# Keys of an attention layer projected with their dimensions on the partitions and rotated there by a partition shuffle

## The chip, the cores and the metric

The kernel runs on one core of a Trainium2 chip. The metric is the device time of one execution in microseconds (us); before the change the median of three runs is 559.24 us (558.02 to 559.66). Engines are called TensorE (PE; its weight loads are PEld), VectorE (DVE), ScalarE (ACT), GpSimd (POOL) and SyncE (SP).

## The reference

Two decoder layers on x of 256 tokens by 1024, all in float32. Each layer normalises x, multiplies it by one combined weight matrix `w_in` and splits the columns into a linear-recurrence group (8 heads, "HGRN2") and a sparse-attention group (8 query heads, 2 groups of keys and values, 128 dimensions a head). The attention has three branches: over compressed keys (blocks of 32 tokens sent through a small MLP, 15 of them), over selected blocks (`ks`, `vs`) and over a window (`kw`, `vw`). Queries, `ks`, `kw` and the compressed keys get a partial rotary embedding over their first 32 of 128 dimensions:

```python
def partial_rope(x, pos):
    ...
    x1 = xf[..., :half]
    x2 = xf[..., half:ROT_DIM]
    out = jnp.concatenate([x1 * cos - x2 * sin, x2 * cos + x1 * sin, xf[..., ROT_DIM:]], axis=-1)
```

The branches' outputs are gated and added, both groups are multiplied by a SiLU gate, projected by `w_out`, normalised and added to x.

## The kernel before, in words

Every float32 product is made of three single-pass products: each operand is split into a high part (cast to `float32r`) and the rest, and hi x hi, hi x lo and lo x hi are accumulated in PSUM. The weights are streamed through a ring (class `Ring`): SP loads a unit into one of 5 raw buffers, ScalarE makes the high part (L202), VectorE the low part (L203), into 8 pairs of buffers. `ring.done(n)` gives n units back and lets SP load the units that lie 8 further on; their splitting is due 9 us of program time later.

TensorE does one projection group after another (`layers`, from L1075 on): queries; the forget gates of the recurrence (`hgrn_fast`, whose scans over 1024 elements run on VectorE); `kcvc`, the inputs of the compression; `kv_w`, keys and values of the window with the gate logits; `compress` for the keys; `kv_s`, keys and values of the selected blocks; `compress` for the values; then the recurrence's queries, with attention woven in between. `mm_a` (L363) has a token tile (128 tokens) as the stationary operand and up to 512 columns of the weights as the moving one, so the tokens end up on the partitions. `mm_b` (L373) has 128 columns of the weights as the stationary operand and all 256 tokens as the moving one, so the dimensions end up on the partitions.

Smaller steps are put off: `later(lag, fn, channel)` sets a due time, `tick` advances a clock by the time of the matmuls emitted and emits what is due, and `flush` forces a channel out. From the order of emission a list scheduler sets the order of each engine's instructions when the program is built, by a timing model of its own; semaphores make an engine wait for its operands and for a buffer's last reader. PSUM has 8 banks: three for the tag `mm`, two each for `s` and `t`, one for `o`; the banks of a tag are handed out in turn.

Keys, before: `keys` (L545) takes a bank with 128 tokens by 2 groups x 128 dimensions, rotates it into the tile `kst` (`rope`, L384: one ScalarE copy of 96 dimensions a group, four VectorE instructions over the first 32), and 8 us later `turn_k` transposes the two groups on TensorE (L552) and `split_k` (L539) writes the high part `kTh` on ScalarE (L540) and the low part `kTl` on VectorE (L541). Each layer does this four times, for two token tiles and two branches. The compressed keys come out of `second` (L514) with their 15 blocks on the partitions (two matmuls, L519), are rotated and transposed in `third` (L531). `vals` (L558) splits a bank of values into `vhi` and `vlo`.

In `kv_s` (L563) one bank of `mm` takes 256 columns of keys and 256 of values for a token tile. In `kv_w` (L574) a token tile's keys go to an `mm` bank (256 columns), its values and gate logits to an `s` bank (280 columns). In both, the four weight units are given back during the second token tile's last pass. `kcvc` (L468), just ahead of `kv_w`, fills two `mm` banks; for each, two copies on ScalarE (L477) and two subtractions on VectorE (L478) follow, one after the other. `scores` (L598) reads `kTh` and `kTl`.

Of the kernel before, what the change touches and what calls it, by code (L numbers as in the profile page):

```python
# [19 lines left out]
T = 256  # L20
# [14 lines left out]
CTW = 544  # L35
# [9 lines left out]
L3 = 3.0  # L45
LQ = 4.0
LK = 8.0
# [5 lines left out]
def shape_tables():  # L53
# [10 lines left out]
    for scale in (SCALE, 1.0):  # L64
        r = rope(t, scale)
        parts.append(r[:128])
        parts.append(r[128:])
    e = 16 * np.arange(NCMP) + 31
    rc = np.zeros((128, 64), np.float32)
    rc[:NCMP] = rope(e, 1.0)  # L70
    parts.append(rc)
# [21 lines left out]
    return f, f2, m  # L93


def build(ctx, tc, A, out):
# [150 lines left out]
    rope_k = [ct[:, 256 + 64 * a:320 + 64 * a] for a in range(NT)]  # L247
    rope_c = ct[:, 384:448]
    cmask = [ct[:, 448 + 16 * a:464 + 16 * a] for a in range(NT)]
    sel = ct[:, 480:540].rearrange("p (a n) -> p a n", a=2)  # L250
# [22 lines left out]
    def consts2():  # L273
# [3 lines left out]
        nc.sync.dma_start(out=m2, in_=A["ct2"])  # L277
        nc.gpsimd.memset(cm3, 0.0)
# [208 lines left out]
    def compress(l, i, ring, KC):  # L487
# [26 lines left out]
        def second():  # L514
            y2 = tb()
            n = 96 if i else NCMP
            for g in range(G):
                lhs = act3[:, g, :] if i else act[:, g * 15:(g + 1) * 15]
                P.matmul(out=y2[0:n, g * 128:(g + 1) * 128], lhsT=lhs, rhs=w2[:, i, :], start=True, stop=True)  # L519
            y2v = y2[0:n, 0:256].rearrange("p (g d) -> p g d", g=2)  # L520
            if i:
                S.copy(out=vcs[0:96], in_=y2v)
                V.tensor_tensor(out=vcs[32:64], in0=y2v[32:64], in1=vcs[32:64].bitcast(F32), op=OP.subtract)
                return
            kst = sp.tile([128, 2, 128], F32, name="kst", tag="st", bufs=2)
            rope(kst[0:NCMP], y2v, rope_c, 2, 1.0, NCMP)

            def third():
                tp = tb()
                for g in range(G):  # L530
                    P.transpose(out=tp[:, g * 128:g * 128 + NCMP], in_=kst[0:NCMP, g, :],  # L531
                                identity=ident[0:NCMP, 0:NCMP])
                split_k(256, NCMP, tp.rearrange("p (g n) -> p g n", g=4)[:, 0:2, 0:NCMP])

            later(L3, third, "c0")
# [7 lines left out]
    KOFF = ((128, 0), (272, 400))  # L543

    def keys(a, br, ps):  # L545
        kst = sp.tile([128, 2, 128], F32, name="kst", tag="st", bufs=2)
        rope(kst, ps.rearrange("p (g d) -> p g d", g=2), rope_k[a], 2, 1.0)

        def turn_k():
            tp = tb()  # L550
            for g in range(G):
                P.transpose(out=tp[:, g * 128:(g + 1) * 128], in_=kst[:, g, :], identity=ident)  # L552
            o = KOFF[br][a]
            split_k(o, 128, tp[:, 0:256].rearrange("p (g t) -> p g t", g=2))

        later(LK, turn_k, "k")

    def vals(a, br, ps):  # L558
        hi, lo = vhi[:, a, br, :], vlo[:, a, br, :]
        S.copy(out=hi, in_=ps)  # L560
        V.tensor_tensor(out=lo, in0=ps, in1=hi.bitcast(F32), op=OP.subtract)

    def kv_s(ring):  # L563
        un = ring.take(4)
        for a in range(NT):
            ps = mmb()
            for u in range(4):
                mm_a(ps, un[u], u, a, 0, 512)
                if a:
                    ring.done(1)  # L570
            keys(a, 0, ps[:, 0:256])
            vals(a, 0, ps[:, 256:512])

    def kv_w(ring):  # L574
        un = ring.take(4)
        for a in range(NT):
            ps = mmb()
            for u in range(4):
                mm_a(ps[:, 0:256], un[u], u, a, 0, 256)
            keys(a, 1, ps[:, 0:256])  # L580
            ps = sb_()
            for u in range(4):
                mm_a(ps[:, 0:280], un[u], u, a, 256, 280)
                if a:
                    ring.done(1)
            vals(a, 1, ps[:, 0:256])
            S.activation(out=gt[:, a].rearrange("p h b -> p (h b)"), in_=ps[:, 256:280], func=AF.Sigmoid)

    def attend(a, g):
# [8 lines left out]
        def scores(i):  # L598
            flush("c0")
# [17 lines left out]
            else:  # L617
                flush("k")
# [556 lines left out]
```

## Time and profile before

| | |
|---|---|
| median of 3 runs | 559.24 us (558.02 to 559.66) |
| the profiled execution | 558.97 us |
| its span, first to last instruction | 557.2 us |
| TensorE busy | 543.8 us (98%) |
| weight loads | 487.6 us (88%) |
| VectorE busy | 398.8 us (72%) |
| ScalarE busy | 333.0 us (60%) |
| mean granted TensorE clock | 0.995 |

The rows below come from the profiled execution; times in them are microseconds from the start of its span, mean durations of a group nanoseconds. A matmul's row lasts longer than the distance to the next matmul, since they are pipelined: the distance between the starts is what a matmul costs.

### The profile page before, as it was taken

Reading aid. Unit: us, or ns where it says so; the run is one execution under the profiler, and the core shown is the slowest. Engines: PE = TensorE matmul, PEld = TensorE weight load, DVE = VectorE, ACT = ScalarE, POOL = GpSimd, SP = SyncE. Lnnn points to the kernel's source line nnn. Section 1 sums busy time; section 2 is a strip of 40 time slices with the busy share of each in tenths; the row PEclk is TensorE's granted clock in tenths of the full one; section 3 lists DMA queues with packets and bytes.
Section 4 is the critical chain, followed back from the end, with each engine's and each line's share of the span. In section 5 each row is a group of like instructions: output and inputs, shape, how many; then the busy total and the mean of one; then the engine's idle time right before and its main releaser. Section 6 shows DMA issues by size and latency. Waiting matters only on the chain.

```text
span 557.2 us, 9821 instructions
## 1 busy us (share of the span) xinstructions
PE 543.8 (98%) x3675; PEld 487.6 (88%) x3675; DVE 398.8 (72%) x883; ACT 333.0 (60%) x632; POOL 9.6 (2%) x18
## 2 busy tenths in 40 slices
PE   7999999999999999999999999989999999999994
PEld 4889998899888989988888999979988888898884
DVE  4887997889777277563687599888987654866422
ACT  6576537865567685562557763677646768746311
POOL 4000000000000001001000000000000000000000
PEclk9999999999999999999999999999999999999998
DMA  8698548965146158566385755697433622956111
GB/s 302 195 314 257 146 127 266 304 193 152 39 117 190 35 166 291 185 191 188 115 262 162 228 154 152 196 302 256 125 101 84 174 85 63 303 172 200 59 38 44
DMA packets 72197, 96.56 MB, mean 173 GB/s; under 512 B 3383, under 2 KB 49357, under 8 KB 72142
## 3 DMA queue, kind: packets, MB, share of 16 engines
q1 hardware_dynamic: 71854, 95.33, 55.2%
q8 instruction: 31, 0.51, 0.4%
q10 hardware_dynamic: 288, 0.52, 0.2%
q14 instruction: 24, 0.20, 0.1%
HBM read 93.75 MB, written 2.10 MB: 172 GB/s over the span
## 4 chain that ended last, share of the span: by engine, by line
PE 88%; DMA 4%; ACT 3%; DVE 2%; issue 1%; SPq 0%; ACTq 0%; DVEq 0%
PE ps_mm L378 10%; PE ps_mm L380 10%; PE ps_mm L379 10%; PE ps_mm L368 9%; PE ps_mm L369 9%; PE ps_mm L370 9%; PE ps_mm L1005 4%; PE ps_mm L1007 4%; PE ps_mm L1006 4%; DMA raw<-in_w_in 2%; ACT whi L202 2%; PE ps_t L668 2%; DMA raw<-in_cmp_w_v 2%; PE ps_s L608 1%; DVE wlo L203 1%
## 5 line engine op out<-in xcount | busy, mean ns | idle before, releaser
L203 DVE TENSOR_TENSOR wlo<-raw,whi 128x1024 fp32r<-128x1024 f32 (+1 forms) x168 | 203.0, 1223 | 60.7 <-ACT whi L202 56.3
L202 ACT CAST whi<-raw 128x1024 fp32r<-128x1024 f32 (+1 forms) x168 | 174.9, 1052 | 87.9 <-PE ps_mm L379 24.5
L378 PE MATMUL ps_mm<-Hhi,whi 128*128 128x256 f32 x448 | 127.5, 285 | 0.0
L380 PE MATMUL ps_mm<-Hhi,wlo 128*128 128x256 f32 x448 | 125.7, 281 | 0.0
L379 PE MATMUL ps_mm<-Hlo,whi 128*128 128x256 f32 x448 | 125.7, 281 | 0.0
L368 PE MATMUL ps_mm<-whi,Hhi 128*128 128x512 f32 (+1 forms) x256 | 102.0, 399 | 0.7 <-ACT Hhi L355 0.7
L370 PE MATMUL ps_mm<-whi,Hlo 128*128 128x512 f32 (+1 forms) x256 | 98.9, 386 | 0.0
L369 PE MATMUL ps_mm<-wlo,Hhi 128*128 128x512 f32 (+1 forms) x256 | 98.8, 386 | 0.0
L379 PEld LDWEIGHTS ps_mm<-Hlo,whi 128*128 128x128 f32 x448 | 84.5, 189 | 0.1
L378 PEld LDWEIGHTS ps_mm<-Hhi,whi 128*128 128x128 f32 x448 | 84.3, 188 | 0.1
L380 PEld LDWEIGHTS ps_mm<-Hhi,wlo 128*128 128x128 f32 x448 | 84.4, 188 | 0.0
L370 PEld LDWEIGHTS ps_mm<-whi,Hlo 128*128 128x128 f32 x256 | 48.7, 190 | 10.3 <-DVE Hlo L356 0.3
L368 PEld LDWEIGHTS ps_mm<-whi,Hhi 128*128 128x128 f32 x256 | 48.9, 191 | 8.5 <-ACT Hhi L355 1.1
L369 PEld LDWEIGHTS ps_mm<-wlo,Hhi 128*128 128x128 f32 x256 | 49.0, 191 | 7.5 <-DVE wlo L203 0.5
L630 ACT ACTIVATE sB<-ps_s,nm 128x256 f32<-128x256 f32 (+1 forms) x40 | 16.9, 428 | 12.2 <-DVE nm L627 11.5
L627 DVE CUSTOM_DVE_ANT_0 ps_s<-ps_s,cm 128x128 f32<-128x128 f32 (+1 forms) x64 | 22.4, 371 | 1.9 <-PE ps_s L610 0.7
L671 DVE TENSOR_TENSOR sB<-ps_t,sB 128x512 fp32r<-128x512 f32 x12 | 8.3, 688 | 20.1 <-ACT sB L670 20.1
L1005 PE MATMUL ps_mm<-whi,sN 128*128 128x512 f32 x48 | 19.0, 397 | 0.0
L1006 PE MATMUL ps_mm<-wlo,Hhi 128*128 128x512 f32 x48 | 18.9, 395 | 0.0
L1007 PE MATMUL ps_mm<-whi,Hlo 128*128 128x512 f32 x48 | 18.9, 395 | 0.0
L1006 PE MATMUL ps_mm<-wlo,sN 128*128 128x512 f32 x48 | 18.9, 394 | 0.0
L1007 PE MATMUL ps_mm<-whi,sN 128*128 128x512 f32 x48 | 18.9, 394 | 0.0
(299 smaller groups left out, 921.0 us busy)
## 6 DMA issues: line engine op xcount, KB each, us to landing
raw<-in_w_in SPq DMA_DIRECT2D x112, 512.0 KB, 4.5
raw<-in_w_out SPq DMA_DIRECT2D x32, 512.0 KB, 4.3
raw<-in_w_in SPq DMA_DIRECT2D x8, 536.0 KB, 4.1
raw<-in_cmp_w_k SPq DMA_DIRECT2D x16, 256.0 KB, 3.4
raw<-in_cmp_w_v SPq DMA_DIRECT2D x16, 256.0 KB, 3.2
sB<-in_x SPq DMA_DIRECT2D x3, 512.0 KB, 3.6
sB<-in_post_norm SPq DMA_DIRECT2D x2, 512.0 KB, 4.8
xs<-sB SPq DMA_DIRECT2D x4, 256.0 KB, 2.0
```

The costliest lines, as they stand in the source:

```text
L202: S.copy(out=hi, in_=raw)
L203: V.tensor_tensor(out=lo, in0=raw, in1=hi.bitcast(F32), op=OP.subtract)
L368: P.matmul(out=ps, lhsT=hh, rhs=wh, start=k == 0, stop=False)
L369: P.matmul(out=ps, lhsT=hh, rhs=wl, start=False, stop=False)
L370: P.matmul(out=ps, lhsT=hl, rhs=wh, start=False, stop=k == KT - 1)
L378: P.matmul(out=ps, lhsT=wh, rhs=hh, start=k == 0, stop=False)
L379: P.matmul(out=ps, lhsT=wh, rhs=hl, start=False, stop=False)
L380: P.matmul(out=ps, lhsT=wl, rhs=hh, start=False, stop=k == KT - 1)
L627: V.tensor_tensor_reduce(out=sb[b], in0=sb[b], in1=mk[b], scale=-1.0, scalar=3e38, op0=OP.add, op1=OP.min, accum_out=nm[:, i, b:b + 1])
L1005: P.matmul(out=ps, lhsT=hi, rhs=wh, start=first, stop=False)
L1006: P.matmul(out=ps, lhsT=hi, rhs=wl, start=False, stop=False)
L1007: P.matmul(out=ps, lhsT=lo, rhs=wh, start=False, stop=last)
```

## The change

Keys are projected with the weights as the stationary operand, as in `mm_b`, for all 256 tokens at once, and come last in their group, behind the values; the tile lies in PSUM with the dimensions on the partitions. The new `rope_t` rotates its first 32 partitions in place: a `stream_shuffle` swaps the two halves of the 32 partitions into an SBUF tile, two multiplications by tables (`kt`, a new constant input with the dimensions on the partitions) and an addition follow, all on VectorE. `split_k` then splits the whole bank at once. `turn` does this 1.5 us after the group instead of 8. The compressed keys are made by one matmul with `w2` stationary, rotated the same way and split at once. The transposes of keys, their `kst` tiles and `third` are gone. Values of `kv_s` now take one `mm` bank for both token tiles; values and gate logits of `kv_w` take an `mm` bank for each. The units of a group are given back in the keys' second half. `scores` flushes the keys' channel at its start.

```diff
-CTW = 544
+CTW = 352
+KTW = 544
...
-L3 = 3.0
 LQ = 4.0
-LK = 8.0
+LR = 1.5
...
         nc.sync.dma_start(out=m2, in_=A["ct2"])
+        nc.sync.dma_start(out=kt, in_=A["kt"])
...
+    def rope_t(x, tab, n):
+
+        c, s = (t[:, None, :].to_broadcast([32, G, n]) for t in tab)
+        sh = sp.tile([128, 512], F32, name="sh", tag="st", bufs=2)[0:32, 0:G * n].rearrange("p (g n) -> p g n", g=G)
+        V.stream_shuffle(out=sh, in_=x[0:32], mask=SWAP)
+        V.tensor_tensor(out=sh, in0=sh, in1=s, op=OP.mult)
+        V.tensor_tensor(out=x[0:32], in0=x[0:32], in1=c, op=OP.mult)
+        V.tensor_tensor(out=x[0:32], in0=x[0:32], in1=sh, op=OP.add)
+
...
         def second():
             y2 = tb()
...
+            if not i:
+                P.matmul(out=y2[:, 0:G * NCMP], lhsT=w2[:, 0, :], rhs=act, start=True, stop=True)
+                y2v = y2[:, 0:G * NCMP].rearrange("p (g n) -> p g n", g=G)
+                rope_t(y2v, rope_c, NCMP)
+                split_k(kTh[:, :, 256:256 + NCMP], kTl[:, :, 256:256 + NCMP], y2v)
+                return
...
-    def split_k(o, n, src):
-        S.copy(out=kTh[:, :, o:o + n], in_=src)
-        V.tensor_tensor(out=kTl[:, :, o:o + n], in0=src, in1=kTh[:, :, o:o + n].bitcast(F32), op=OP.subtract)
...
+    def split_k(hi, lo, src):
+        S.copy(out=hi, in_=src)
+        V.tensor_tensor(out=lo, in0=src, in1=hi.bitcast(F32), op=OP.subtract)
+
+    def keys(un, br, ring):
+        ps = mmb()
+        for g in range(G):
+            out = ps[:, g * T:(g + 1) * T]
+            for k in range(KT):
+                wh, wl = (t[:, k % 2, g * 128:(g + 1) * 128] for t in un[k // 2])
+                P.matmul(out=out, lhsT=wh, rhs=Hhi[:, :, k, :], start=k == 0, stop=False)
+                P.matmul(out=out, lhsT=wh, rhs=Hlo[:, :, k, :], start=False, stop=False)
+                P.matmul(out=out, lhsT=wl, rhs=Hhi[:, :, k, :], start=False, stop=k == KT - 1)
+                if g and k % 2:
+                    ring.done(1)
+                tick(3 * 256 / 2400.0)
+
+        def turn():
+            rope_t(ps.rearrange("p (g t) -> p g t", g=G), rope_k, T)
+            if br:
+                split_k(kTh[:, :, 272:528], kTl[:, :, 272:528], ps.rearrange("p (g t) -> p g t", g=G))
+            else:
+                hi, lo = (t[:, :, 0:256].rearrange("p g (a t) -> p g a t", a=NT)[:, :, ::-1, :] for t in (kTh, kTl))
+                split_k(hi, lo, ps.rearrange("p (g a t) -> p g a t", g=G, a=NT))
+
+        later(LR, turn, "k")
...
     def kv_s(ring):
         un = ring.take(4)
+        ps = mmb()
         for a in range(NT):
-            ps = mmb()
             for u in range(4):
-                mm_a(ps, un[u], u, a, 0, 512)
-                if a:
-                    ring.done(1)
-            keys(a, 0, ps[:, 0:256])
-            vals(a, 0, ps[:, 256:512])
+                mm_a(ps[:, a * 256:(a + 1) * 256], un[u], u, a, 256, 256)
+        vals(vhi[:, :, 0, :], vlo[:, :, 0, :], ps.rearrange("p (a d) -> p a d", a=NT))
+        keys(un, 0, ring)
 
     def kv_w(ring):
         un = ring.take(4)
         for a in range(NT):
             ps = mmb()
             for u in range(4):
-                mm_a(ps[:, 0:256], un[u], u, a, 0, 256)
-            keys(a, 1, ps[:, 0:256])
-            ps = sb_()
-            for u in range(4):
                 mm_a(ps[:, 0:280], un[u], u, a, 256, 280)
-                if a:
-                    ring.done(1)
-            vals(a, 1, ps[:, 0:256])
+            vals(vhi[:, a, 1, :], vlo[:, a, 1, :], ps[:, 0:256])
             S.activation(out=gt[:, a].rearrange("p h b -> p (h b)"), in_=ps[:, 256:280], func=AF.Sigmoid)
+        keys(un, 1, ring)
...
         def scores(i):
-            flush("c0")
+            flush("c0", "k")
```

## Rows read from the trace of the kernel before

**Rows 1.** The page's parts 1 and 5: TensorE as a whole, one group of weight loads

```profile
PE 543.8 (98%) x3675; PEld 487.6 (88%) x3675; DVE 398.8 (72%) x883; ACT 333.0 (60%) x632; POOL 9.6 (2%) x18
...
L378 PEld LDWEIGHTS ps_mm<-Hhi,whi 128*128 128x128 f32 x448 | 84.3, 188 | 0.1
```

**Rows 2.** Timeline of TensorE, `kv_w` in both layers: start, duration, instruction, [idle before]

```profile
72.18 0.28 PE L368 MATMUL ps_mm<-whi,Hhi 128*128 128x256 f32 x1
...
75.02 0.29 PE L368 MATMUL ps_s<-whi,Hhi 128*128 128x280 f32 x1
...
78.11 0.28 PE L368 MATMUL ps_mm<-whi,Hhi 128*128 128x256 f32 x1
...
340.22 0.28 PE L368 MATMUL ps_mm<-whi,Hhi 128*128 128x256 f32 x1
```

**Rows 3.** Timeline of TensorE, first token tile of `kv_s` in the first layer

```profile
87.98 0.39 PE L368 MATMUL ps_mm<-whi,Hhi 128*128 128x512 f32 x1
...
90.54 0.39 PE L370 MATMUL ps_mm<-whi,Hlo 128*128 128x512 f32 x1
90.78 0.38 PE L552 MATMUL ps_t<-ct,kst 128*128 128x128 f32 x2
...
91.23 0.40 PE L369 MATMUL ps_mm<-wlo,Hhi 128*128 128x512 f32 x1
```

**Rows 4.** Timeline of VectorE: the last split of each `kcvc` bank, both layers

```profile
75.53 0.60 DVE L478 TENSOR_TENSOR sN<-ps_mm,sN 128x256 fp32r<-128x256 f32 x1
...
80.23 0.63 DVE L478 TENSOR_TENSOR sN<-ps_mm,sN 128x256 fp32r<-128x256 f32 x1
...
341.53 0.63 DVE L478 TENSOR_TENSOR sN<-ps_mm,sN 128x256 fp32r<-128x256 f32 x1
...
348.91 0.63 DVE L478 TENSOR_TENSOR sN<-ps_mm,sN 128x256 fp32r<-128x256 f32 x1
```

**Rows 5.** Timeline of TensorE around `third` (L531), inside `compress` for the values

```profile
102.55 0.28 PE L493 MATMUL ps_s<-wlo,sN 128*68 128x256 f32 x1
...
103.81 0.28 PE L493 MATMUL ps_s<-wlo,sN 128*68 128x256 f32 x1
...
370.65 0.28 PE L493 MATMUL ps_s<-wlo,sN 128*68 128x256 f32 x1
372.33 0.27 PE L531 MATMUL ps_t<-ct,kst 15*128 15x15 f32 x2 [1.40 <-ACT whi L202]
...
372.70 0.28 PE L493 MATMUL ps_s<-wlo,sN 128*68 128x256 f32 x1
372.81 0.28 PE L492 MATMUL ps_s<-whi,sN 128*68 128x256 f32 x1
```

**Rows 6.** Timeline of TensorE: the first scores of the first layer

```profile
114.04 0.28 PE L608 MATMUL ps_s<-kTh,q 128*128 128x272 f32 x1
```

**Rows 7.** Timeline of TensorE around the two matmuls of `second` (L519), first layer

```profile
98.22 0.40 PE L370 MATMUL ps_mm<-whi,Hlo 128*128 128x512 f32 x1
...
99.42 0.40 PE L369 MATMUL ps_mm<-wlo,Hhi 128*128 128x512 f32 x1
```

**Rows 8.** Timeline of TensorE: first dense matmuls of the kernel, and its last one

```profile
9.63 0.79 PE L368 MATMUL ps_mm<-whi,Hhi 128*128 128x512 f32 x1 [0.69 <-ACT Hhi L355]
...
15.45 0.63 PE L368 MATMUL ps_mm<-whi,Hhi 128*128 128x512 f32 x1
15.88 0.43 PE L369 MATMUL ps_mm<-wlo,Hhi 128*128 128x512 f32 x1
...
549.42 0.27 PE L1007 MATMUL ps_s<-whi,Hlo 128*128 128x256 f32 x1
```

**Rows 9.** Busy time by stretch: PE, PEld, DVE, ACT, POOL, granted clock, DMA share, GB/s

```profile
551.50:552.00 0.50, 0.00 (x0) 0.00 (x0) 0.50 (x3) 0.00 (x0) 0.00 (x0) 0.84 0.07 16
```

**Rows 10.** Groups of VectorE's instructions by line and shape: count, busy us, mean ns

```profile
L825 DVE TENSOR_TENSOR sB<-ps_mm,sB 128x512 f32<-128x512 f32 x4 | 2.8, 688 | 0.3 <-PE ps_mm L380 0.3
```

**Rows 11.** Timeline of SP's queue: the issue of the constant table

```profile
2.01 0.43 SPq L271 DMA_DIRECT2D ct<-in_ct  x1
```

More of the change, by code (lines that the diff above doesn't have):

```diff
@@ L63, in shape_tables @@
     parts = [np.eye(128, dtype=np.float32)]
[L64 to L67, printed above, removed]
+    r = rope(t, SCALE)
+    parts.append(r[:128])
+    parts.append(r[128:])
     e = 16 * np.arange(NCMP) + 31
-    rc = np.zeros((128, 64), np.float32)
-    rc[:NCMP] = rope(e, 1.0)
-    parts.append(rc)
     for a in range(NT):
@@ L92, in shape_tables @@
     m = np.ascontiguousarray(np.concatenate(ms, axis=1).astype(np.float32))
-    return f, f2, m
+    rows = [r[:, i:i + 32].T for r in (rope(t, 1.0), rope(e, 1.0)) for i in (0, 32)]
+    kt = np.concatenate(rows, axis=1).astype(np.float32)
+    kt = np.ascontiguousarray(np.pad(kt, ((0, 0), (0, KTW - kt.shape[1]))))
+    return f, f2, m, kt
 def build(ctx, tc, A, out):
@@ L246, in build @@
     rope_q = [ct[:, 128 + 64 * a:192 + 64 * a] for a in range(NT)]
[L247 to L250, printed above, removed]
+    cmask = [ct[:, 256 + 16 * a:272 + 16 * a] for a in range(NT)]
+    sel = ct[:, 288:348].rearrange("p (a n) -> p a n", a=2)
+    kt = cp.tile([32, KTW], F32, name="kt")
+    rope_k = (kt[:, 0:256], kt[:, 256:512])
+    rope_c = (kt[:, 512:512 + NCMP], kt[:, 512 + NCMP:512 + 2 * NCMP])
+    SWAP = [(i + 16) % 32 for i in range(32)]
     cm3 = cp.tile([128, 384], BF, name="cm3")
@@ L515, in second @@
             y2 = tb()
-            n = 96 if i else NCMP
-            for g in range(G):
[L518 to L535, printed above, removed]
@@ L537, in compress @@
-        later(L1[i], sums, "c%d" % i)
-    def split_k(o, n, src):
-        S.copy(out=kTh[:, :, o:o + n], in_=src)
-        V.tensor_tensor(out=kTl[:, :, o:o + n], in0=src, in1=kTh[:, :, o:o + n].bitcast(F32), op=OP.subtract)
[L543 to L556, printed above, removed]
@@ L558, in vals @@
-    def vals(a, br, ps):
-        hi, lo = vhi[:, a, br, :], vlo[:, a, br, :]
+            if not i:
[4 more added lines that the diff above has]
+                return
+            for g in range(G):
+                P.matmul(out=y2[0:96, g * 128:(g + 1) * 128], lhsT=act3[:, g, :], rhs=w2[:, i, :], start=True,
+                         stop=True)
@@ new lines, in second @@
+            y2v = y2[0:96, 0:256].rearrange("p (g d) -> p g d", g=2)
+            S.copy(out=vcs[0:96], in_=y2v)
+            V.tensor_tensor(out=vcs[32:64], in0=y2v[32:64], in1=vcs[32:64].bitcast(F32), op=OP.subtract)
+        later(L1[i], sums, "c%d" % i)
+    def split_k(hi, lo, src):
[21 more added lines that the diff above has]
+        later(LR, turn, "k")
@@ L560, in vals @@
+    def vals(hi, lo, ps):
         S.copy(out=hi, in_=ps)
@@ L617, in scores @@
             else:
-                flush("k")
                 qk(ps[:, 0:272], 0, 272)
@@ L1166 @@
     arrays = {n: np.ascontiguousarray(inputs[n]) for n in _INS}
-    arrays["ct"], arrays["ct2"], arrays["lm"] = shape_tables()
+    arrays["ct"], arrays["ct2"], arrays["lm"], arrays["kt"] = shape_tables()
     A = {n: nc.dram_tensor("in_" + n, a.shape, mybir.dt.from_np(a.dtype), kind="ExternalInput").ap()
```

## The prediction

> **What bounds the kernel now.** I read the page first: TensorE is busy for 543.8 of 557.2 us [rows 1]. That figure alone is weak, since a matmul's row (0.28 us) is longer than the distance to the next one, so I went to the timeline of TensorE through the stage that is changed. There the matmuls of 256 columns start 0.118 us apart ((75.02 - 72.18)/24) and those of 280 columns 0.129 us ((78.11 - 75.02)/24 = 3.09/24) [rows 2]; those of 512 columns start 0.233 us apart ((90.54 - 87.98)/11) [rows 3]. So the distance goes with the columns, and between these groups there is no gap. Whatever takes columns or interruptions from TensorE shortens the kernel one for one, and whatever makes TensorE wait lengthens it one for one. VectorE comes second, and locally it is late: in `kv_w`'s stretch it still works off the gate scans when TensorE has long gone on, and gets to the evacuation of the step before only then [rows 4].
>
> **What the change removes.** (a) Eight pairs of 128x128 transposes (`turn_k`, four a layer). One pair: from the start of the matmul before it, 90.54, to the second start after it, 91.23, are 0.69 us; without the pair two distances of 0.233 would stand there, so a pair costs 0.22 us, and eight cost 1.8 us [rows 3].
> (b) The transposes of the compressed keys (`third`) and the wait ahead of them. In the first layer the starts go from 102.55 to 103.81 us where two distances of 0.118 belong: 1.02 us. In the second layer they go from 370.65 to 372.70, a loss of 1.81 us, of which 1.40 is a wait [rows 5]. TensorE no longer has a step there, so both go: 2.8 us. What was late there, the rotation of the compressed keys, is now awaited only by the first scores, which start at 114.04 us [rows 6].
> (c) `second` for the keys runs two matmuls of 128 columns, each in two passes; it becomes one of 30 columns. Today it lifts the distance from 98.22 to the second matmul behind it, 99.42, to 1.20 us, 0.73 more than the plain 0.467 [rows 7]. The new cost lies between nothing and 0.73; half as many passes make me take half, so 0.37 is saved in each layer, 0.7 in both (0 to 1.5).
>
> **What it adds on TensorE.** `kv_s` exchanges 48 matmuls of 512 columns for 96 of 256 in each layer: 96 x 0.118 - 48 x 0.233 = 0.15 us, 0.3 in both layers [rows 2, 3]. `kv_w` keeps its 48 of 256 and 48 of 280 columns in another order. The Trainium skill speaks against this exchange: "TensorE: Matmul & The Clock Gate", section "Back-to-back issue gap", gives about 81 ns for a matmul of 128 columns and about 131 ns for one of 512 in a stream of weight loads and matmuls; put on a line between them (an estimate), 256 columns would take 98 ns, and the exchange would lose some 6 us over both layers. The trace doesn't agree: it shows 118 and 233 ns, very nearly in proportion.
>
> So TensorE's own work falls by 1.8 + 2.8 + 0.7 - 0.3 = **5.0 us**.
>
> **What it turns into a wait.** `kv_w` used to alternate between the `mm` banks (keys) and the `s` banks (values). Now three tiles in a row come from `mm`, which has three banks, handed out in turn. When `kv_w` starts, one of them is free, and the other two hold the output of `kcvc`. They come free when their last split on VectorE (L478) ends, and ScalarE and VectorE take the four steps of each evacuation one by one, behind the scans. These ends stand in the trace: 75.53 + 0.60 = 76.13 and 80.23 + 0.63 = 80.86 us in the first layer, 341.53 + 0.63 = 342.16 and 348.91 + 0.63 = 349.54 in the second [rows 4]. Before, the second `mm` tile began at 78.11 [rows 2] and the third only in `kv_s`, at 87.98 [rows 3], so nobody waited.
> Now, first layer: values of tile 0 from 72.18 for 3.09 us to 75.27; values of tile 1 wait 0.86 us for 76.13 and end at 79.22; keys wait 1.64 us for 80.86. Second layer: start 340.22 [rows 2], values to 343.31 and 346.40 (the bank of 342.16 is free in time), then keys wait 3.14 us for 349.54. Together 5.6 us. The VectorE work ahead of these two splits isn't touched by the change, so I take the times as they are. Bounds: 0, if the order of VectorE's instructions comes out with the splits first, and 5.6.
>
> A further price hangs on it. The clock granted to TensorE falls after a pause: the last matmul starts at 549.42, and the half microsecond from 551.50 is granted 0.84 on average, so it has gone to the lower level (1.2 GHz) some 2.4 us after the last start [rows 8, 9]. A wait of 1.40 us left no such mark: the matmuls right behind it keep their distance [rows 5]. The new wait of 3.1 us is longer than both, those of 0.9 and 1.6 us are near the harmless one. What the lower clock costs until it comes back: nothing at the least; at the most what the start of the kernel shows, where matmuls of 512 columns run 0.43 us apart (15.45 to 15.88), half the pace, from 9.63 to 15.88, which loses 6.25/2 = 3.1 us [rows 8]. I take the middle, 1.55 us, once, for the second layer.
>
> **What is hidden.** Each branch's rotation on VectorE becomes four instructions over 32 partitions and 512 elements, and one split of 512. The nearest row, 128x512 out of PSUM, takes 0.69 us [rows 10], so a branch takes at most 5 x 0.69 = 3.4 us, and with ScalarE's copy about 4. The shuffle itself is in no row: its bounds are nothing and, as I can't exclude it, twice that row, which makes a branch 4.1 us. The Trainium skill ("VectorE: DVE Perf Modes", section "Rules for kernel authors") has about 2400 ns for 2048 elements, an estimate of 0.6 us here; by it the sum stays. The cover is the time from the end of `kv_s` to the first scores: at 102.55 TensorE is already in the `compress` behind `kv_s` [rows 5], the scores start at 114.04 [rows 6], so 11.5 us at least, less 1.5 us of due time. If it were gone, what ran over would stand ahead of the first scores. Behind these steps on VectorE are weight splits of units that TensorE takes after `compress`. The units of `kv_s` are now given back in its last quarter instead of its second half, up to 3 us later; they let loads start whose data are wanted a whole projection group later: nothing. The extra table costs SP one issue of about 0.43 us, as the other table [rows 11], ahead of loads that stand in a queue behind the weight buffers anyway; the other table gets smaller: nothing either, 0.4 us at most if that cover went.
>
> **Sum.** The profiled execution took 558.97 us, its span 557.2; the median of the runs is 559.24, 0.27 above, and I add to the median. -5.0 + 5.6 + 1.55 = +2.2 us: **561.4 us**.
>
> **Rivals.** (1) *The banks come free in time.* The order of VectorE's instructions is set when the program is built; if the two splits of the second `kcvc` half come ahead of the last scan and the products, there's no wait, and 559.24 - 5.0 = 554.2 us is left: faster. For it: the splits wait in VectorE's queue, not for data. Against it: nothing ahead of them changes, and the order was the same kind in both layers [rows 4]. It decides once more than about 3.3 of the 5.6 us of waiting go. Chance 0.30.
> (2) *The wait comes, the clock stays.* 559.24 + 0.6 = 559.9 us. For it: the harmless 1.40 us [rows 5]. Against it: the fall after the last matmul [rows 8, 9]. Chance 0.20.
> (3) *VectorE becomes the bound*: the rotation of `kw`'s keys, 3.4 us, comes ahead of the splits of the last two weight units of `kv_s`, which TensorE now wants sooner, as its 256-column pass goes through a unit in 0.7 us. That would cost up to the 3.4 us in each layer on top of (2), less what the wait has given: about 563 us. Chance 0.04.
> (4) *Short matmuls are bound by their weight loads*: a load lasts 188 ns [rows 1]; if the new 96 a layer ran at that distance, 2 x 96 x (0.188 - 0.118) = 13 us more. Against it: the same form runs at 0.118 now [rows 2]. It's what the skill's figures point to, in a smaller size. Chance 0.02.
> The forecast keeps 0.44.
>
> **The numbers.** About 0.3% (1.7 us) is what a measurement of this kernel can tell from no change, so faster means below 557.6 and slower above 560.9. Faster: rival (1), 0.30. Same: three quarters of (2), and a fifth of the forecast, where the clock costs little, 0.24. Slower: the rest, 0.46. Both signs hold much, so the range spans them: from just under rival (1), 554.0, to just over the wait with the full price of the clock (559.9 + 3.1), 563.2. The forecast's own range is 559.9 to 563.0.
>
> **What would show it.** In the new trace: no transposes of keys; a gap of about 2.5 us in all ahead of the `kv_w` keys' matmuls in the first layer and of about 3 us in the second, released by L478's successor on VectorE; behind the second gap a stretch of the lower clock. Keys' matmuls 0.118 us apart. The scores still begin without a wait. If the gaps are missing and the span is near 552, the step on the banks is wrong; if they stand there and the clock does not fall, only its price is.

## The result and the profile after

After takes 563.16 us (median of 9 executions, 562.03 to 566.86), before 558.55 us (9 executions beside them); the ratio is 1.0085, with a 95% interval from 1.0064 to 1.0106. By the ratio the change costs 4.7 us. The profiled execution of after took 563.62 us, its span 561.8 us, 4.6 more than before.

The page of the kernel after: busy time of each engine [rows 1], and the group of the keys' matmuls.

```profile
PE 541.2 (96%) x3747; PEld 490.2 (87%) x3747; DVE 402.5 (72%) x867; ACT 331.3 (59%) x616; POOL 9.6 (2%) x18
...
L552 PE MATMUL ps_mm<-Hhi,whi 128*128 128x256 f32 x64 | 18.3, 286 | 4.4 <-DVE sN L489 4.4
```

TensorE is busy for 2.6 us less, but its share of the span falls: work went, waits came. The keys' matmuls alone have 4.4 us of idle time ahead of them, ended by the last split of `kcvc` on VectorE (L489, formerly L478). They stand in the timeline of TensorE after, in `kv_w` of both layers (columns as in [rows 2]).

```profile
75.45 0.29 PE L372 MATMUL ps_mm<-whi,Hlo 128*128 128x280 f32 x1
76.57 0.37 PE L370 MATMUL ps_mm<-whi,Hhi 128*128 128x280 f32 x1 [0.83 <-DVE sN L489]
...
79.61 0.29 PE L372 MATMUL ps_mm<-whi,Hlo 128*128 128x280 f32 x1
81.25 0.36 PE L552 MATMUL ps_mm<-Hhi,whi 128*128 128x256 f32 x1 [1.34 <-DVE sN L489]
81.44 0.28 PE L553 MATMUL ps_mm<-Hlo,whi 128*128 128x256 f32 x1
81.56 0.28 PE L554 MATMUL ps_mm<-Hhi,wlo 128*128 128x256 f32 x1
...
348.48 0.29 PE L372 MATMUL ps_mm<-whi,Hlo 128*128 128x280 f32 x1
351.82 0.36 PE L552 MATMUL ps_mm<-Hhi,whi 128*128 128x256 f32 x1 [3.04 <-DVE sN L489]
```

From start to start these three gaps are 1.12, 1.64 and 3.34 us where 0.13 belongs, 5.7 us lost in all. The keys' matmuls that follow are 0.12 us apart. A second kind of wait comes at the third of the first scores, in the same view.

```profile
119.61 0.28 PE L382 MATMUL ps_mm<-Hhi,wlo 128*128 128x256 f32 x1
121.02 0.39 PE L611 MATMUL ps_s<-kTh,q 128*128 128x272 f32 x1 [1.13 <-ACT sN L632]
...
390.16 0.28 PE L382 MATMUL ps_mm<-Hhi,wlo 128*128 128x256 f32 x1
391.99 0.39 PE L611 MATMUL ps_s<-kTh,q 128*128 128x272 f32 x1 [1.55 <-ACT sN L632]
```

It was not there before, where the third scores follow on at once:

```profile
118.64 0.28 PE L380 MATMUL ps_mm<-Hhi,wlo 128*128 128x256 f32 x1
118.76 0.29 PE L608 MATMUL ps_s<-kTh,q 128*128 128x272 f32 x1
...
387.51 0.28 PE L380 MATMUL ps_mm<-Hhi,wlo 128*128 128x256 f32 x1
387.62 0.29 PE L608 MATMUL ps_s<-kTh,q 128*128 128x272 f32 x1
```

The starts of the first matmul of each stage, read from the same timeline, give each stage's length. "Values in `s`" and "rotation later" are variants of after that are told of below (first and twelfth experiment).

| stage, first / second layer, us | before | after | values in `s` | and rotation later |
|---|---|---|---|---|
| `kv_w` | 11.99 / 12.11 | 14.48 / 15.13 | 11.85 / 11.85 | 11.85 / 11.85 |
| `compress`, keys | 3.81 / 3.76 | 3.71 / 3.71 | 3.72 / 3.71 | 3.71 / 3.72 |
| `kv_s` | 12.61 / 12.60 | 12.39 / 12.34 | 13.75 / 14.34 | 12.03 / 12.70 |
| `compress`, values | 4.96 / 5.75 | 3.68 / 3.70 | 3.70 / 3.69 | 3.68 / 3.69 |
| recurrence's queries, first scores | 31.05 / 31.13 | 32.03 / 32.46 | 31.88 / 31.93 | 31.91 / 31.05 |
| sum | 64.42 / 65.35 | 66.29 / 67.34 | 64.90 / 65.52 | 63.18 / 63.01 |

So in after the five stages lose 3.9 us over both layers: `kv_w` +5.5, the two `compress` -3.5, `kv_s` -0.5, the first scores' stage +2.3. The other stages keep their lengths to 0.1 us. The remaining 0.7 us of the span lies ahead of `kv_w` (it starts at 72.50 instead of 72.18) and in the tail; in the kernels below, which are alike up to there, `kv_w` starts between 70.6 and 73.2, so that part says nothing of the change.

The timeline of VectorE after tells where the scores' wait comes from: the rotation of `kv_s`, then weight splits (L202), then the softmax of the first scores (L627, L629).

```profile
103.29 0.73 DVE L390 STREAM_SHUFFLE sh<-ps_mm 32x512 f32<-32x512 f32 x1
103.93 0.68 DVE L392 TENSOR_TENSOR ps_mm<-ps_mm,kt 32x512 f32<-32x512 f32 x1
104.53 0.67 DVE L391 TENSOR_TENSOR sh<-sh,kt 32x512 f32<-32x512 f32 x1
105.13 1.21 DVE L202 TENSOR_TENSOR wlo<-raw,whi 128x1024 fp32r<-128x1024 f32 x1
106.26 0.68 DVE L393 TENSOR_TENSOR ps_mm<-ps_mm,sh 32x512 f32<-32x512 f32 x1
106.86 1.20 DVE L202 TENSOR_TENSOR wlo<-raw,whi 128x1024 fp32r<-128x1024 f32 x1
108.39 0.69 DVE L544 TENSOR_TENSOR kTl<-ps_mm,kTh 128x512 fp32r<-128x512 f32 x1 [0.33 <-ACT kTh L543]
109.00 4.62 DVE L202 TENSOR_TENSOR wlo<-raw,whi 128x1024 fp32r<-128x1024 f32 x4
...
116.11 1.23 DVE L202 TENSOR_TENSOR wlo<-raw,whi 128x1024 fp32r<-128x1024 f32 x1 [0.75 <-ACT whi L201]
117.25 0.17 DVE L627 TENSOR_TENSOR pc<-ps_s,ct 128x16 f32<-128x16 f32 x1
117.75 1.23 DVE L202 TENSOR_TENSOR wlo<-raw,whi 128x1024 fp32r<-128x1024 f32 x1 [0.34 <-ACT whi L201]
118.89 0.29 DVE L629 CUSTOM_DVE_ANT_0 ps_s<-ps_s,cm 128x128 f32<-128x128 f32 x1
```

TensorE starts the last matmul of the first scores at 115.26 us, but the minimum over them (L629), for which the exponential and so the bank wait, starts at 118.89, behind splits that themselves wait. A raw weight buffer comes free when its split is done, so a late split also makes a load late. That this goes back to the rotation is so far read from the order of these rows; experiments 5, 12, 13 and 17 test it.

### The profile page after: what moved, and what is told of

Read it like the earlier page. It is cut to its first block, busy times and chain, and to the rows that moved or that the text cites. A ratio compares the mean times of both kernels' runs of the same rounds, so it can differ in the third digit from the quotient of the medians.

```text
span 561.8 us, 9928 instructions
## 1 busy us (share of the span) xinstructions
PE 541.2 (96%) x3747; PEld 490.2 (87%) x3747; DVE 402.5 (72%) x867; ACT 331.3 (59%) x616; POOL 9.6 (2%) x18
## 4 chain that ended last, share of the span: by engine, by line
PE 78%; DVE 11%; DMA 5%; issue 3%; ACT 2%; SPq 0%; DVEq 0%; ACTq 0%
PE ps_mm L370 9%; PE ps_mm L371 9%; PE ps_mm L372 9%; PE ps_mm L380 5%; PE ps_mm L381 5%; PE ps_mm L382 5%; DVE wlo L202 5%; DMA raw<-in_w_in 5%; PE ps_mm L1008 4%; PE ps_mm L1007 4%; PE ps_mm L1009 4%; PE ps_t L670 2%; PE ps_mm L552 1%; ACT whi L201 1%; PE ps_s L611 1%
## 5 line engine op out<-in xcount | busy, mean ns | idle before, releaser
L202 DVE TENSOR_TENSOR wlo<-raw,whi 128x1024 fp32r<-128x1024 f32 (+1 forms) x168 | 202.7, 1222 | 60.8 <-ACT whi L201 58.1
L380 PE MATMUL ps_mm<-Hhi,whi 128*128 128x256 f32 x448 | 127.2, 284 | 0.0
L370 PE MATMUL ps_mm<-whi,Hhi 128*128 128x512 f32 (+2 forms) x256 | 98.3, 385 | 2.2 <-ACT Hhi L357 1.4
L371 PE MATMUL ps_mm<-wlo,Hhi 128*128 128x512 f32 (+2 forms) x256 | 95.6, 374 | 0.1
L372 PE MATMUL ps_mm<-whi,Hlo 128*128 128x512 f32 (+2 forms) x256 | 95.2, 372 | 0.0
L629 DVE CUSTOM_DVE_ANT_0 ps_s<-ps_s,cm 128x128 f32<-128x128 f32 (+1 forms) x64 | 22.4, 371 | 2.4 <-PE ps_s L613 1.3
L552 PE MATMUL ps_mm<-Hhi,whi 128*128 128x256 f32 x64 | 18.3, 286 | 4.4 <-DVE sN L489 4.4
L1007 PE MATMUL ps_mm<-whi,sN 128*128 128x512 f32 x48 | 19.1, 397 | 0.0
```

Source lines behind the costliest of these rows:

```text
L202: V.tensor_tensor(out=lo, in0=raw, in1=hi.bitcast(F32), op=OP.subtract)
L370: P.matmul(out=ps, lhsT=hh, rhs=wh, start=k == 0, stop=False)
L371: P.matmul(out=ps, lhsT=hh, rhs=wl, start=False, stop=False)
L372: P.matmul(out=ps, lhsT=hl, rhs=wh, start=False, stop=k == KT - 1)
L552: P.matmul(out=out, lhsT=wh, rhs=Hhi[:, :, k, :], start=k == 0, stop=False)
L1007: P.matmul(out=ps, lhsT=hi, rhs=wh, start=first, stop=False)
```

## The experiments

Before was timed beside each; its medians were 558.7 to 559.7 us. The interval behind a ratio to before is the 95% one. First come the two waits.

**1. Values of `kv_w` in the `s` banks again**

```diff
 def kv_w(ring):
...
     for a in range(NT):
-        ps = mmb()
+        ps = sb_()
```

> The changed kernel, with kv_w's values back in the s banks, so that only its keys take an mm bank. Theory (TensorE waits for mm banks in kv_w, 2.5 us in the first layer and 3.2 in the second, and that time is a pure addition): both waits vanish, 563.2 - 5.7 = 557.5 us, and the scores in the queries' group still wait some 1.3 and 1.7 us. Rival (the wait only shields TensorE from VectorE, which is late anyway; without it the same time is lost at compress or in kv_s, waiting for weight splits): 562 to 563 us.

Measured: 559.76 us, ratio 1.0005 (0.9991 to 1.0019), between the theory and the rival. `kv_w` falls to 11.85 us in both layers, so the bank waits are gone. But a new wait stands in `kv_s`, in TensorE's timeline:

```profile
88.86 0.28 PE L370 MATMUL ps_mm<-whi,Hhi 128*128 128x256 f32 x1
89.56 0.39 PE L371 MATMUL ps_mm<-wlo,Hhi 128*128 128x256 f32 x1 [0.42 <-DVE wlo L202]
...
90.25 0.28 PE L370 MATMUL ps_mm<-whi,Hhi 128*128 128x256 f32 x1
91.29 0.39 PE L371 MATMUL ps_mm<-wlo,Hhi 128*128 128x256 f32 x1 [0.77 <-DVE wlo L202]
```

and VectorE's timeline of the same kernel shows who holds the two splits up:

```profile
84.18 2.36 DVE L202 TENSOR_TENSOR wlo<-raw,whi 128x1024 fp32r<-128x1024 f32 x2 [1.20 <-ACT whi L201]
86.46 0.01 DVE L390 LOAD_MASK_SELECT sh<-ps_mm  x1
86.46 0.73 DVE L390 STREAM_SHUFFLE sh<-ps_mm 32x512 f32<-32x512 f32 x1
87.10 0.68 DVE L392 TENSOR_TENSOR ps_mm<-ps_mm,kt 32x512 f32<-32x512 f32 x1
87.70 0.67 DVE L391 TENSOR_TENSOR sh<-sh,kt 32x512 f32<-32x512 f32 x1
88.30 1.20 DVE L202 TENSOR_TENSOR wlo<-raw,whi 128x1024 fp32r<-128x1024 f32 x1
89.43 0.68 DVE L393 TENSOR_TENSOR ps_mm<-ps_mm,sh 32x512 f32<-32x512 f32 x1
90.03 1.20 DVE L202 TENSOR_TENSOR wlo<-raw,whi 128x1024 fp32r<-128x1024 f32 x1
```

The rotation of `kv_w`'s keys stands ahead of the splits of the last two units that `kv_s` is already asking for. ScalarE's casts for these two splits end at 86.04 and 86.99, so the splits wait for nothing but their turn on VectorE. That is the place that rival (3) named. At the third scores the wait goes on (0.99 and 1.03 us).

**2. Early give-back** (units of `kv_s` given back from 62% of the group on; for that the keys are accumulated in two banks, and the rotation goes in two halves)

```diff
-    keys(un, 0, ring)
+    kp = [mmb(), mmb()]
+    for k in range(KT):
+        for g in range(G):
+            ...
+            if g and k % 2:
+                ring.done(1)
```

> The changed kernel, with the keys of kv_s accumulated in two banks with the weight rows outermost, so that its four weight units are given back from 62% of the stage on, as before the change, and not from 81% on. Theory (the units given back late let the loads for the recurrence's second query group land 2 to 3 us later; ScalarE and VectorE, in order, stand at their splits, the first scores' softmax comes behind them, and TensorE waits for an s bank): the scores' waits go, about 2.3 us over both layers, 560.9 us; the bank waits of kv_w stay. Rival (the softmax is late because the rotation adds work to VectorE): the rotation is the same work in more instructions, so 563 us or a little more.

Measured: 564.17 us, 1.0097 (1.0076 to 1.0117). The wait at the third scores falls from 1.13 and 1.55 us to 0.26 and none, but smaller ones come further on (0.34 and 0.22, 0.33 and 0.27), and the scores' stage stays at 32.35 and 31.82 us: the 2.3 us that the theory expected don't come back. Since the rotation is halved too, this run alone does not tell what the give-back does to the wait.

**3. Both of these**

```diff
-        ps = mmb()
+        ps = sb_()
...
-    keys(un, 0, ring)
+    kp = [mmb(), mmb()]
```

> Both edits: values of kv_w in s banks and the early give-back in kv_s. Theory: the two losses are independent, 563.2 - 5.7 - 2.3 = 555.2 us, that is 3.4 us under the kernel before. Rivals: as in the two single runs; if the waits only move, 560 us or more.

Measured: 559.58 us, 1.0012 (0.9996 to 1.0027), with the waits of the first.

**4. Before, with a late give-back**

```diff
-                if a:
-                    ring.done(1)
+                if a and u > 1:
+                    ring.done(2)
```

> The kernel before, with only the give-back of kv_s's four units put off to 87.5% and 100% of the stage, two at a time; nothing of the new projection in it. Theory (the late give-back alone makes the first scores wait): 558.6 + 1.5 to 3 us, with a wait of TensorE at the third or fourth scores. Rival (the rotation on VectorE is the cause): 558.6 us, no such wait.

Measured: 559.18 us, 1.0003 (0.9985 to 1.0021), scores' stage 31.06 and 31.12. A give-back at least as late as that of after costs nothing in before, and an earlier one gains no time in after (2, 3): the theory that the give-back makes the scores late falls.

The next question: is it the rotation on VectorE, or does TensorE simply go through the units too fast?

**5. Without the rotation of the token keys** (on top of 1)

```diff
-            rope_t(ps.rearrange("p (g t) -> p g t", g=G), rope_k, T)
```

> The variant with the values of kv_w in the score banks (559.8 us, level with before), with the rotation of the token keys left out: no shuffle, no three tensor_tensors (4 x 0.69 us of VectorE a branch, four branches); the keys are only split, so the output is that of unrotated keys. If the rotation's block on VectorE is what makes the weight splits late, the waits for wlo inside kv_s (1.2 us in layer 0, 1.8 in layer 1) go, kv_s falls from 13.8 and 14.3 to 12.4, and the stage of the first scores falls from 31.9 to about 31.1: 555 to 556 us. If the weights are late because TensorE now asks for units faster than they are split (0.7 us a unit in the values pass against 1.22 us of VectorE for one split), the waits stay near 1 us a layer and the scores still wait: 558.5 to 559.8.

Measured: 555.86 us, 0.9935 (0.9912 to 0.9959), 3.9 us less than 1 by the two ratios; no wait above 0.4 us is left in `kv_s` (12.03 and 12.65 us). It is the rotation that costs the 3.9 us. At the third scores waits of 0.52 and 0.78 us are left; the keys' split and ScalarE's copy still stand in their early place here.

**6. Before, with the compressed keys alone done the new way**

```diff
...
+            if not i:
+                P.matmul(out=y2[:, 0:G * NCMP], lhsT=w2[:, 0, :], rhs=act, start=True, stop=True)
+                y2v = y2[:, 0:G * NCMP].rearrange("p (g n) -> p g n", g=G)
+                rope_t(y2v, rope_c, NCMP)
+                split_k(256, NCMP, y2v)
+                return
...
```

> The kernel before with the compressed keys alone done the new way (one matmul, rotated on the partitions, no third step); token keys as before, with their transposes. The sum of the prediction gives it 2.8 + 0.7 us and no new bank wait: 555.7. If that wait was time in which ScalarE and VectorE caught up with the weight splits, part of it comes back as a wait at the first scores, 0.5 to 1 us a layer: 556.7 to 558.

Measured: 558.51 us, 0.9993 (0.9975 to 1.0011): a smaller gain than either column has. The step's 2.8 us in the two `compress` stages go, but in the second layer TensorE's next step that needs ScalarE waits instead:

```profile
374.44 0.28 PE L385 MATMUL ps_mm<-Hhi,wlo 128*128 128x256 f32 x1
376.54 0.52 PE L518 MATMUL ps_t<-ct,st 68*128 68x30 f32 x3 [1.82 <-ACT st L513]
```

**7. First scores 3 us later** (on top of 1)

```diff
-PW = 7.0
+PW = 10.0
```

> The variant with the values of kv_w in the score banks, and the attention begun 3 us later in TensorE's order (PW 10 for 7). If the first scores wait only because the exp behind them stands in line after weight splits that are late at that moment, three more microseconds of matmuls ahead of them take most of the 1.0 us a layer away: about 558. If the backlog is a matter of the stage as a whole, the wait stays or moves on: 559.8.

Measured: 560.42 us, 1.0029 (1.0007 to 1.0051). The scores' waits halve (0.35 and 0.56 us, from 0.99 and 1.03), those in `kv_s` stay, and no time is gained. In the profiled execution `kv_s` of the second layer takes 15.92 us instead of 14.34: behind the same waits as in 1 (1.02 and 0.77 us) the granted clock is 0.50 from 363 to 365 us, where in 1 it stays at 1.00.

**8. Units asked for in turn**

```diff
...
             for u in range(4):
                 mm_a(ps[:, a * 256:(a + 1) * 256], un[u], u, a, 256, 256)
+                keys_u(kp, un, u, a)
+                if a:
+                    ring.done(1)
...
```

> After, with the two passes over the units mixed: for each unit the values of one token tile and the keys of one head group, so that a unit is asked for every 1.4 us as before and given back from the first unit of the second pass on; values of kv_w in the score banks, keys in one mm bank. If the waits for wlo in kv_s come from TensorE asking for units twice as fast, kv_s is 12.4 without a wait, kv_w 11.9, and what is left is the scores' wait of about 1 us a layer: 556 to 557. If the rotation's block makes the splits late, the waits stay somewhere in kv_s or the compression of the values: 559 to 560.

Measured: 562.33 us, 1.0045 (1.0022 to 1.0067); the profiled execution took 559.51 us, the lowest of eight. The median is above both columns. The waits for `wlo` go, as the first column has it, but a wait of 0.71 and 2.56 us for the sums of the compressed keys (<-ACT st L510) comes into `kv_s`: ScalarE's copy stands behind its casts of late weights. Behind the longer one the granted clock is 0.56 and 0.59 in the two stretches of 2 us from 361 on, and `kv_s` of the second layer takes 16.39 us. Asking more slowly doesn't free the line; the wait changes its name.

Now amount against place of VectorE's work.

**9. Before, with more VectorE work**

```diff
+    junk = cp.tile([128, 512], F32, name="junk")
...
+            if a:
+                for i in range(3):
+                    V.tensor_tensor(out=junk, in0=junk, in1=junk, op=OP.mult)
             o = KOFF[br][a]
```

> The kernel before with nothing of the change in it, but with three more tensor_tensors of 128x512 on VectorE (about 0.69 us each) ahead of the split of the second key tile of each branch: 4.1 us more VectorE work a layer, on data that nothing reads. Leaving the rotation out took 4.7 us of VectorE a layer away and 3.9 us of the time. If VectorE, with the weight splits in its line, bounds the stretch from kv_w to the first scores, the added work costs about as much: 3 to 7 us more than before, with TensorE waits for wlo or ahead of the first scores. If VectorE has slack there, as the prediction's cover of 11.5 us says: within 0.5 us of before.

Measured: ratio 1.0012 (0.9994 to 1.0031), and in the profile every stage as in before (`kv_s` 12.61 and 12.61, scores 31.05 and 31.12 us). The added group has 12 instructions, 690 ns each, in all 8.3 us, close to the 9.3 us that 5 took away; here they cost nothing that can be told from noise. The amount alone isn't the cause.

**10. Products of the recurrence on GpSimd** (on top of 1)

```diff
+        E = nc.gpsimd if c else V
...
-            V.tensor_tensor(out=K, in0=K, in1=Q, op=OP.mult)
+            E.tensor_tensor(out=K, in0=K, in1=Q, op=OP.mult)
...
```

> The variant with the values of kv_w in the score banks, with three products of the hidden state's second chain (one of 128x1024, two of 128x512, 1.22 + 0.69 + 0.69 us of VectorE, in line among the splits during kv_w) on GpSimd instead. The rotation and its place are untouched. If VectorE's work in this stretch is the bound, taking 2.6 us a layer out of its line takes most of the waits in kv_s (1.2 and 1.8 us) away: 556 to 557.5. If it is the rotation's place or the weight stream, nothing changes: 559.8. If GpSimd and VectorE hinder each other, or the products come late, it is above 560.

Measured: 563.31 us, 1.0071 (1.0048 to 1.0094), the third column. The timelines of GpSimd and, below, VectorE in this kernel:

```profile
74.15 2.41 POOL L800 TENSOR_TENSOR sB<-sB,sB 128x1024 f32<-128x1024 f32 x1 [67.69 <-PE ps_s L372]
76.64 1.92 POOL L814 TENSOR_TENSOR sB<-sB,ce 128x512 f32<-128x512 f32 x1
78.53 2.02 POOL L817 TENSOR_TENSOR sB<-sB,kx 128x512 f32<-128x512 f32 x1
```

```profile
74.45 5.20 DVE L202 TENSOR_TENSOR wlo<-raw,whi 128x1024 fp32r<-128x1024 f32 x2
```

While GpSimd works, two weight splits take 5.20 us instead of 2.36 (x2 in the rows of 1). The Trainium skill, "SBUF — State Buffer", section "Who interferes with whom", says that a VectorE instruction with two inputs in SBUF contends with a GpSimd instruction that reads SBUF; these rows agree, 1.4 us a split. `kv_s` takes 16.42 and 15.91 us, and part of that is the clock: it is granted at 0.50 from 92 to 95 and from 362 to 364 us. The two executions with the highest mean clock (0.995) still take 561.27 and 561.55 us. Nothing follows from this run for the amount.

**11. The same move in before**

```diff
+        E = nc.gpsimd if c else V
...
-            V.tensor_tensor(out=K, in0=K, in1=Q, op=OP.mult)
+            E.tensor_tensor(out=K, in0=K, in1=Q, op=OP.mult)
...
```

> The kernel before with the same three products on GpSimd: the control for that move. Before has TensorE waits only around the third step of the compressed keys (1.0 and 1.8 us) in this stretch. If they come from VectorE's line: 557 to 558.5. If not: 558.7, as before.

Measured: 561.33 us, 1.0033 (1.0014 to 1.0051): the move alone is a loss.

**12. The rotation later** (on top of 1)

```diff
-LR = 1.5
+LR = 8.0
```

> The variant with the values of kv_w in the score banks, with the rotation due 8 us after its matmuls in place of 1.5 (the age at which the kernel before split its keys). If only the place of the rotation's block ahead of the last splits for kv_s does the harm, the waits in kv_s go and the time is 557 to 558. If the amount of VectorE's work is the bound, the waits move to the compression of the values or to the first scores: 559 to 560.5.

Measured: 555.89 us, 0.9936 (0.9915 to 0.9956): by the ratios 3.9 us less than 1, with all the work still done, and lower than the first column has it. VectorE's timeline, the same stretch as in 1:

```profile
84.89 5.77 DVE L202 TENSOR_TENSOR wlo<-raw,whi 128x1024 fp32r<-128x1024 f32 x5 [1.20 <-ACT whi L201]
90.58 0.01 DVE L390 LOAD_MASK_SELECT sh<-ps_mm  x1
90.58 0.73 DVE L390 STREAM_SHUFFLE sh<-ps_mm 32x512 f32<-32x512 f32 x1
```

Five splits run in one stretch, and the rotation comes behind them. TensorE goes through `kv_s` of the first layer without a gap (12.03 us). A small wait for `kTl` comes at the first scores there (0.33 us), and one for ScalarE's copy `st` in `kv_s` of the second layer (0.43 us, 12.70 us in all). ScalarE's copy of the block moves with the rotation here; in 5 it stays, and the time is the same, so it is not that copy. Together with 5 and 9 this settles it for this variant: the place of the block, not its size.

**13. After itself, rotation later**

```diff
-LR = 1.5
+LR = 8.0
```

> After with one number changed: both rotations due 8 us after their matmuls in place of 1.5; values of kv_w stay in the mm banks. The bank waits in kv_w come from the evacuation of the compressed keys' sources and not from the rotation, so they stay (2.5 and 3.2 us). If place is a loss of its own beside them, the scores' waits (1.0 and 1.3 us) and the small one in kv_s go: 560.5 to 561.5. If in after the bank waits themselves give VectorE the time that the rotation needs, the move brings nothing: 563.

Measured: 561.87 us, 1.0037 (1.0016 to 1.0057). The scores' stage falls from 32.03 and 32.46 us to 31.23 and 31.24, `kv_s` from 12.39 and 12.34 to 12.03 in both; the waits for banks stay to the hundredth (0.83, 1.34, 3.04 us). So the two losses of after are separate. Both blocks move here, so this run doesn't tell the blocks apart.

**14 to 16. The two blocks apart** (on top of 1; due times for `kv_s` and `kv_w`)

```diff
-LR = 1.5
+LR = (8.0, 12.0)
...
-        later(LR, turn, "k")
+        later(LR[br], turn, "k")
```

> Values of kv_w in the score banks; the rotation of kv_w due 12 us after its matmuls, that of kv_s 8 us. The move to 8 and 8 gave 555.9 and left a first-score wait of 0.9 us in layer 0 alone. If kv_w's block needs only to stand behind the splits of the compressed values' weights, 12 is as good as 8: 555.5 to 556.2. If it now falls into the compression of the values or the hq stage and holds up their splits: 556.5 to 558.

Measured: 556.37 us, 0.9937 (0.9915 to 0.9960). The first layer's scores' stage is 30.75 us, without a wait, the second's 32.64 with two (1.29 and 0.51), and in `kv_s` of the second layer stands a wait for `st` (1.21): no gain.

```diff
+LR = (4.0, 8.0)
```

> Values of kv_w in the score banks; the rotation of kv_w due after 8 us, that of kv_s after 4, so that the split of kv_s's keys is done before the first scores ask for them. If the wait of 0.5 us inside the first scores of layer 0 (for kTl) is all that is left, it goes: 555 to 555.6. If an earlier block holds up the hq splits instead: 556 to 557.5.

Measured: 555.57 us, 0.9931 (0.9909 to 0.9954), the lowest, but no different from 12. The number is the theory's by luck: the wait for `kTl` that was to go is still there (0.33 us), with one for `st` in `kv_s` of the second layer (0.94 us).

```diff
+LR = (1.5, 8.0)
```

> Values of kv_w in the score banks; the rotation of kv_w due after 8 us, that of kv_s after 1.5 as in the change. It tells the two blocks apart: if kv_w's block alone does the harm (it stands ahead of splits that kv_s waits for), the time is 555.5 to 556.5 with no wait in kv_s; if kv_s's block, ahead of the hq splits, does as much: 557.5 to 558.5, with the scores' wait of about 1 us a layer.

Measured: 556.69 us, 0.9943 (0.9921 to 0.9964), just above the first column. `kv_s` has no wait for `wlo` (in the second layer one of 1.43 us for `st`), but the third scores wait 2.30 and 0.69 us in the profiled execution (558.04 us, the highest of six). By the ratios `kv_w`'s block is worth 3.5 of the 3.9 us and `kv_s`'s 0.4, with intervals as wide as that; by the stages of that one execution `kv_s`'s is worth the larger part. Both do harm; how much each is not settled.

The best version is thus the change with the values of `kv_w` in the `s` banks and the rotations due after 8 us, that of `kv_s` after 8 or 4: 0.6% to 0.7% below before.

## Why the prediction was right or wrong

The direction was right, the size was not: 2.2 us more were forecast, and by the medians it is 4.6. That 563.16 us still lies just inside the range that ends at 563.2 is luck: that end was reached by the full price of the clock, which after's median execution doesn't pay, and the loss came from a term that had been put at nothing.

**TensorE's saving (5.0 us): right,** about 5.4. The two `compress` stages save 3.5 us in after: (b), 2.8, with the pairs of transposes of (a) that stood in them or at their edge (in before at 84.04, 104.87, 352.08 and 373.75 us). The rest is seen where a stage is free of waits or nearly so: `kv_w` 0.1 and 0.3 (1), `kv_s` 0.6 each (13), the scores' stage 0.3 (15) and 0.1 (12). (c) lies in `kv_s` and saves more than was taken: in after the starts around its matmul go from 100.61 to 101.07 us, 0.22 more than two distances of 0.118, where before it was 0.73. That is 0.5 a layer. Experiment 6 adds that (b) and (c) bring little by themselves, 0.4 us (none to 1.4 within the interval): the wait of the second layer turned up one step on.

**Waits for `mm` banks (5.6 us): right,** in place, releaser and size: 0.86 + 1.64 + 3.14 were forecast, 1.0 + 1.5 + 3.2 lost. Rival (1) falls. (Its threshold was also worked out wrongly: it wins once the waits left are below 3.3 us, that is when more than 2.3 of the 5.6 go, not 3.3. The price of rival (2) is 559.8 by its own sum, not 559.9.)

**The clock (1.55 us): right as a range, but not one number.** In the profiled execution of after nothing was lost behind the wait of 3.04 us: this is rival (2) in that respect. In those of experiments 2 and 13 the same wait brought the lower clock, at 1.5 and 2.7 us. The mean granted clock of each execution is on record: of after's nine, the two longest (564.86 and 566.86 us) have the lowest, 0.989, and the median one has 0.997, as the profiled one; in 13 the three at 0.995 or above take 559.3 to 560.1 us, the nine at 0.993 or below 561.5 to 563.3.

**What is hidden: wrong, and this is the step that failed.** The block's size was right: 0.73 us for the shuffle, three times 0.68, 0.69 for the split, 3.5 us in all. Its cover was measured against the reader of its result, the scores. But VectorE's instructions run in the order that was set when the program was built, and what matters is who stands behind the block. "Behind these steps on VectorE are weight splits of units that TensorE takes after `compress`" was not true of `kv_w`'s block, due 1.5 us after its matmuls: `kv_s`'s own last two splits stood behind it (1). And behind `kv_s`'s block stood splits that put off the softmax of the first scores, so that "The scores still begin without a wait" held for the first two and not for the third. (That in after it is `kv_s`'s block is read from the timeline; in 17, where that block alone is early, the third scores wait 2.30 and 0.69 us.) Rival (3) had the first half of this, at 3.4 us a layer and a chance of 0.04; the runs give 3.9 us for both layers when there is no bank wait. In after `kv_s` begins some 3 us later, behind the bank waits, and is only 0.4 and 0.3 us longer than in 13; most of the loss is that of the scores' stage, 2.3 us, of which the later due time takes 2.0 back (13). In the prediction's own terms the five stages give -5.4 (saving) + 5.9 (bank waits: gaps of 5.7, and slower first matmuls behind them) + 0 (clock, in this execution) + 3.4 (what was put at nothing: 2.7 in the scores' stage and 0.7 in `kv_s`, each against its length without the wait) = +3.9 us.

**Late give-back, nothing: right** for the time (2, 3 and 4). **Short matmuls bound by their loads: no;** the 256-column matmuls of the keys run 0.12 us apart.

Two points are open. The clock goes with part of the scatter of after's executions (562.0 to 566.9 us), but only those with the lowest mean clock stand out; the three at 0.992 and 0.993 take no longer than the four at 0.997 and 0.998, and what decides whether a wait brings the lower clock is not shown. And what sets the wait that is left at the first scores, now in one layer, now in the other (14 to 16), wasn't settled.

## What to carry to other kernels

Ask of every step that is moved who is queued behind it on its engine, and when that one is due, before you ask when its own result is wanted; two blocks of 3.5 us a layer on VectorE cost 2 us a layer in one place, and 6.5 us later the kernel was as fast as without the rotation. When tiles move from one pool of PSUM banks to another, read from the trace when the bank they inherit is last read. And a wait that goes away may only have been the first to meet a late engine: look for the next step that needs it.

## What was not expected of the hardware

The same wait leaves the clock alone in one execution and lowers it in another. The granted clock (the figure behind the five engines' busy times and counts) by stretches of 2 us, first the kernel after, whose wait ends at 351.82, then experiment 2, whose wait of equal length ends at 350.48, then 13, where it ends at 349.50:

```profile
350.00:352.00 2.00, 0.18 (x1) 0.21 (x2) 1.91 (x4) 0.83 (x2) 0.00 (x0) 1.00 0.72 248
352.00:354.00 2.00, 2.00 (x18) 2.00 (x18) 2.00 (x4) 0.46 (x2) 0.00 (x0) 1.00 0.00 1
```

```profile
350.00:352.00 2.00, 1.52 (x10) 1.55 (x11) 2.00 (x4) 0.45 (x2) 0.00 (x0) 0.78 0.22 84
352.00:354.00 2.00, 2.00 (x11) 2.00 (x11) 0.72 (x2) 0.19 (x1) 0.00 (x0) 0.50 0.09 27
```

```profile
350.00:352.00 2.00, 2.00 (x12) 2.00 (x11) 1.75 (x3) 0.64 (x3) 0.00 (x0) 0.50 0.01 4
352.00:354.00 2.00, 2.00 (x11) 2.00 (x11) 0.00 (x0) 0.00 (x0) 0.00 (x0) 0.50 0.65 194
```

In the second the first matmuls behind the wait still start 0.12 us apart, then, from 351.14 to 354.55, 0.213 us, the pace of 1.2 GHz instead of 2.4. `kv_w` of the second layer takes 15.13, 16.64 and 17.87 us in the three. Shorter waits show the same: behind those of 1.02 and 0.77 us in `kv_s` of the second layer the clock is lower in 7 and stays at 1.00 in 1.

An instruction of VectorE over 32 partitions cost here what one over 128 did: 0.68 us for 512 elements, beside 0.69 in [rows 10]. So this rotation on a quarter of the partitions wasn't cheaper for it: a branch takes 3.5 us in five instructions where ten smaller ones took 2 x (0.22 + 0.18 + 0.18 + 0.22 + 0.42) = 2.4 us before, and VectorE's busy time rose by 3.7 us in all. The shuffle's 0.73 us stands beside the estimate of 0.6 that the prediction made from the Trainium skill, "VectorE: DVE Perf Modes", section "Rules for kernel authors".
